# Expert down products ordered chunk by chunk, the further places' products in one run behind, and the end's row loads and register loads reordered

## The chip, the cores and the metric

The kernel runs on one core of a Trainium2 chip, as one program launched once. The metric is the device time in microseconds (us). A core has a matrix engine (PE, with a queue of its own for loading weights, PEld), a vector engine (DVE), a scalar engine (ACT), a general engine (POOL) and a queue that issues transfers (SP); each takes its instructions in its own program order and waits for the others by semaphores. Transfers between the chip's memory (HBM) and the core's buffers run on 16 DMA engines.

## What is computed

One layer on 2048 tokens of 1024 features: two linear-attention mixers, an output projection, and a mixture of experts, with a last normalization. The change touches the experts and the end.

```python
def hier_moe(h, ...):              # h: tokens x 1024, normalized
    # each token goes to its 2 best of the 8 experts in its best of 4 groups
    ...
    def expert_block(args):
        xb, e = args
        return (jax.nn.silu(xb @ w_gate[e]) * (xb @ w_up[e])) @ w_down[e]
    ...
    out = jax.ops.segment_sum(ys * row_w[:, None], row_tok, num_segments=n_tok)

x = x + hier_moe(rmsnorm(x, ln2_w), ...)
return rmsnorm(x, ln_f_w)
```

There are 32 experts. `w_gate` and `w_up` are 1024 x 512 each, `w_down` is 512 x 1024, all in 32-bit floats.

## The kernel before

The stages ahead of the experts (mixers, output projection, routing) end at about 1780 us and are the same in both kernels. They leave the normalized tokens in HBM as two 16-bit halves (`sH`), the residual rows (`sX2`), and for each expert a list of its tokens.

**Precision.** Each 32-bit factor is held as a high and a low 16-bit half, and a product is three matmuls: high x high, high x low, low x high.

**Weights.** `weights_of` (L1292 to L1306) brings an expert's weights in six pieces of 1 MB: gate 0 and 1, up 0 and 1, down 0 and 1. A piece is loaded by SP into one of four buffers `wr` (L1299) and split in two steps: ACT writes the high half into `whl` (L120), DVE the low half (L121), which needs ACT's. The `whl` pieces go round fourteen buffers of 8 KB per partition, six in one pool and eight in another. While PE works on one expert, ACT and DVE split the next one's pieces.

**Places.** An expert has 160 places: 128 in a tile `xg` and 32 further ones in `xg2`, where a token's row lies as four quarters on four partitions. Both are gathered by POOL (L1376, L1380). A token beyond 160 would go to a loop behind the experts (`overflow()` prepares it at expert 3; in this data the loop's body is not run).

**One expert** (`expert`, L1383 to L1449):

- tr: PE transposes the tokens (L1393, and L1401 for `xg2`); ACT copies the high halves into `hTm`, DVE the low ones (L1395, L1402).
- gu: for each of four chunks m of 128 hidden features, 48 matmuls (24 gate, 24 up; L1413) add into one of two buffers `gu`. ACT takes the silu (L1417), DVE multiplies by up (sgm, L1418), ACT writes the high half `ah` (L1419), DVE the low half `al` (L1420).
- dn: for the 128 places, two halves n of 512 output columns, 12 matmuls each (L1429): three products of four chunks. ACT empties n = 0 (L1432), DVE n = 1 (yt, L1434), and POOL scatters `yt` to `sYb` (L1365).
- dr: for the 32 further places, 48 matmuls (L1443), each with 32 columns of weights and 256 moving columns; four of them, for the four quarters of the output, lie side by side in the array. ACT empties them into `yr` (L1447), POOL scatters them.

**What sets the order.** The loop (L1482 to L1493) calls `expert(e)` as a generator and pulls pieces of `weights_of(e + 1)` between its steps. A scheduler then orders the instructions of each engine by a timeline model of its own, among all that depend on nothing unfinished. `tc.issue_after(i)` tells it to place what follows behind instruction i on the engine's queue. So dn and dr of one expert are mixed with tr and gu of the next.

**The end.** When all experts are placed, the weights' buffers are freed, and eight tiles `xr` of the residual (1 MB each, two tiles of 128 tokens) and the last norm's weights `lfb` are loaded into their place (L1501 to L1504). Then each engine loads the overflow loop's count into a register (`values_load`, L1511) and comes to the loop's branch (L1512), at which the engines and the transfers are waited for. Behind it `summed` and `finish` read both expert results of each token (`yf`, L1530, 16 loads of 1 MB), add them to `xr` on DVE (L1532, L1533), normalize (L1535, L1540) and write the result.

Of the kernel before, what the change touches and what calls it, by code (L numbers as in the profile page):

```python
# [9 lines left out]
F32 = mybir.dt.float32  # L10
# [3 lines left out]
AF = mybir.ActivationFunctionType  # L14
# [6 lines left out]
D = 1024  # L21
NT = T // 128
# [22 lines left out]
def tile_kernel(ctx, tc, I, out, dbg=None, stop=99):  # L45
    nc = tc.nc
    V, S, G, P = nc.vector, nc.scalar, nc.gpsimd, nc.tensor
# [19 lines left out]
    sX2 = dram.tile([NT, 128, D], F32, name="sX2")  # L67
# [175 lines left out]
    with pool("p0", 2) as p0:  # L243
# [13 lines left out]
        for t in range(NT):  # L257
# [24 lines left out]
            if t == TV:  # L282

                rows = p0.tile([NV, 128], F32, name="vrows", bufs=1)
                for nme, n in VECS:
                    o = VOFF[nme]
                    a = I[nme]
# [516 lines left out]
    f, b = slice(0, 64), slice(64, 128)  # L804
# [487 lines left out]
    def weights_of(e, res, dyn=False):  # L1292


        for i, (nme, kt) in enumerate((("moe_w_gate", 4), ("moe_w_up", 4), ("moe_w_down", 2))):
            src = I[nme][0, e] if not dyn else I[nme][0, bass.ds(e, 1)].rearrange("o k f -> (o k) f")
            for c in range(2):
                wr = mp["wq"].tile([128, 2048], F32, name="wr")
                nc.sync.dma_start(wr.rearrange("p (k f) -> p k f", k=kt),  # L1299
                                  src[c * kt * 128:(c + 1) * kt * 128, :].rearrange("(k p) f -> p k f" if i == 2 else "(p k) f -> p k f", p=128))  # L1300
                whl = mp["wsp"][next(wpl) % len(mp["wsp"])].tile([128, 2, 2048], F16, name="whl")
                wh, wl = whl[:, 0], whl[:, 1]
                for q in range(2):
                    o = slice(1024 * q, 1024 * q + 1024)
                    split(wh[:, o], wl[:, o], wr[:, o])
                    yield  # L1306
                res.append(tuple(z.rearrange("p (k f) -> p k f", k=kt) for z in (wh, wl)))

    wts = []
# [32 lines left out]
    if True:  # L1342
# [5 lines left out]
        def tokens(dst, src):  # L1348
            V.tensor_scalar(dst, src, T - 1, None, op0=ALU.bitwise_and)
# [12 lines left out]
        ysc = []  # L1362

        def scatter(dst, ix, src, bound):
            ins = G.indirect_dma_start(out=dst, out_offset=bass.IndirectOffsetOnAxis(ap=ix, axis=0), in_=src, in_offset=None,  # L1365
                                       bounds_check=bound, oob_is_err=False)
            for o in ysc:
                tc.declare_no_dep(ins.ins, o.ins, reason="rows of different places")
            ysc.append(ins)

        last = {}
# [11 lines left out]
        def expert(wts, xs, sc, sc2=None):  # L1383

            xg, x2 = xs
            nt = 128 if x2 is None else 160
            hT = mw.tile([128, 2, 8, 160], F16, name="hTm")
            for a in range(2):
                for kq in range(2):
                    pt = ms.tile([128, 4, 128], F16, name="tr")  # L1390
                    for k in range(4):
                        c = a * D + kq * 512
                        P.transpose(pt[:, k, :], xg[:, c + k:c + 512:4], idh)  # L1393
                    o = hT[:, a, kq * 4:kq * 4 + 4, 0:128]
                    ins = S.activation(o, pt, AF.Copy) if a == 0 else V.tensor_copy(o, pt)  # L1395
                last["AV"[a]] = ins.ins
                if a == 0 and x2 is not None:

                    pt = ms.tile([128, 4, 128], F16, name="tr")
                    for j in range(4):  # L1400
                        P.transpose(pt[:, j, :], x2[:, j::4], idh)  # L1401
                    last["A"] = S.activation(hT.rearrange("p a (g j) t -> p (a g) j t", j=4)[:, :, :, 128:160],  # L1402
                                             pt.rearrange("p j (q r) -> p q j r", r=32), AF.Copy).ins
                yield
            ah = mw.tile([128, 4, 160], F16, name="ah")
            al = mw.tile([128, 4, 160], F16, name="al")
            for m in range(4):
                pg = ms.tile([128, 2, 160], F32, name="gu")
                for i in range(2):
                    j = 0  # L1410
                    for a, hf in ((0, 0), (0, 1), (1, 0)):
                        for k in range(8):
                            P.matmul(pg[:, i, 0:nt], wts[2 * i + k // 4][a][:, k % 4, m * 128:(m + 1) * 128], hT[:, hf, k, 0:nt],  # L1413
                                     start=(j == 0), stop=(j == 23))
                            j += 1
                sg = mw.tile([128, 160], F32, name="sgm")
                S.activation(sg[:, 0:nt], pg[:, 0, 0:nt], AF.Silu, scale=IS2)  # L1417
                V.scalar_tensor_tensor(sg[:, 0:nt], pg[:, 1, 0:nt], IS2 * ASC, sg[:, 0:nt], op0=ALU.mult, op1=ALU.mult)  # L1418
                last["A"] = S.activation(ah[:, m, 0:nt], sg[:, 0:nt], AF.Copy).ins  # L1419
                last["V"] = V.tensor_tensor(al[:, m, 0:nt], sg[:, 0:nt], ah[:, m, 0:nt], op=ALU.subtract).ins  # L1420
                yield
            ym = cq.tile([128, 2, NP, 128], F32, name="yt").rearrange("p d q t -> p (d q t)")
            dn = 1.0 / (ASC * SW)
            for n in range(2):
                pd = ms.tile([128, 512], F32, name="dn")
                j = 0
                for a, b in ((ah, 0), (al, 0), (ah, 1)):
                    for m in range(4):
                        P.matmul(pd, a[:, m, 0:128], wts[4 + m // 2][b][:, m % 2, n * 512:(n + 1) * 512], start=(j == 0), stop=(j == 11))  # L1429
                        j += 1  # L1430
                if n == 0:
                    last["A"] = S.activation(ym[:, 0:512], pd, AF.Copy, scale=dn).ins  # L1432
                else:
                    last["V"] = V.tensor_scalar(ym[:, 512:1024], pd, dn, None, op0=ALU.mult).ins  # L1434
                yield
            scatter(sYb[:, :], sc, ym, 2 * T - 1)
            if x2 is not None:
                pd = ms.tile([128, 256], F32, name="dr", bufs=1)
                j = 0
                for a, b in ((ah, 0), (al, 0), (ah, 1)):  # L1440
                    for m in range(4):
                        for n in range(4):
                            P.matmul(pd[32 * n:32 * n + 32, :], a[:, m, 128:160], wts[4 + m // 2][b][:, m % 2, n * 256:(n + 1) * 256],  # L1443
                                     start=(j == 0), stop=(j == 11), skip_group_check=True)
                        j += 1
                yr = mw.tile([128, 256], F32, name="yr")
                S.activation(yr, pd, AF.Copy, scale=dn)  # L1447
                scatter(sY4, sc2, yr, 8 * T - 1)
            yield  # L1449

# [31 lines left out]
        for e in range(32):  # L1482
# [9 lines left out]
            wts = nxt  # L1492
# [3 lines left out]
        p6.close()  # L1496

        fx = p5.enter_context(pool("fx"))
        xr = []
        lfb = fx.tile([128, D], F32, name="lfb")  # L1500
        nc.sync.dma_start(lfb, bcast(I["ln_f_w"], D))  # L1501
        for t in range(0, NT, 2):
            xr.append(fx.tile([128, 2, D], F32, name=f"xr{t}"))
            load = nc.sync.dma_start(xr[-1], sX2[t:t + 2].rearrange("t p d -> p t d"))  # L1504


        with ExitStack() as p7:
            mp["wq"] = p7.enter_context(pool("wqo", 2))
            mp["wsp"] = [p7.enter_context(pool("wspo", 6))]
            with tc.issue_after(load.ins):  # L1510
                nbr = nc.values_load(ovl[0:1, 2, 0:1], min_val=0, max_val=63)  # L1511
            with tc.For_i(0, nbr, 1) as iv:  # L1512
                er = nc.values_load(ovl[0:1, 0, bass.ds(iv, 1)], min_val=0, max_val=31)
                br = nc.values_load(ovl[0:1, 1, bass.ds(iv, 1)], min_val=0, max_val=NSLOT - 128)
                ido = mw.tile([128, 1], I32, name="ido")
                nc.sync.dma_start(ido, sT[bass.ds(br, 128), bass.ds(er, 1)])
                tko = mw.tile([128, 1], I32, name="tko")
                tokens(tko, ido)
                wts = []
                for _ in weights_of(er, wts, True):  # L1520
                    pass
                for _ in expert(wts, gather(tko), ido):
                    pass
# [57 lines left out]
```

## Time and profile before

| | |
|---|---|
| runs | 2589.75, 2592.13, 2596.44 us; median 2592.13 |
| the profiled execution | 2596.26 us, of which the trace spans 2594.5 |
| instructions | 57329 |
| mean granted TensorE clock | 0.913 |
| from HBM / to HBM | 420.94 MB / 168.66 MB |
| expert loop, from its first gate product to the last dr | 1782.97 to 2503.80 us |
| end, from there to the last instruction | 2503.80 to 2594.5 us |
| chain that ended last, largest parts | PE gu 12%, PE dn 4%, ACT whl 3%, DVE whl 3%, PE dr 1% |

A row of a timeline has the start in us, the duration, the engine (SPq is SP's issuing), the line, the operation, output<-input, the shape, and how many instructions the row holds; in brackets stands how long the engine was idle before it, and who ended that. Matmuls are pipelined and their ends are modelled, so the time of a matmul is best read from one start to the next.

### The profile page before, as it was taken

How to read it: one execution, taken by the hardware profiler on the slowest of the kernel's cores; microseconds unless marked ns; L12 is line 12 of the kernel's file. 1: busy time of each engine (PE TensorE's matmuls, PEld its weight loads, DVE VectorE, ACT ScalarE, POOL GpSimd, SP SyncE). 2: the span in 40 equal slices, each digit the busy share in tenths (PEclk: the TensorE clock that was granted, in tenths of full speed). 3: DMA queues.
4: the chain of work that ended last, by engine and by line, in shares of the span. 5: the costliest groups of instructions: out<-in, count | busy, mean ns of one | idle time of the engine just before them, and what ended most of it. 6: DMA issues, size and time to landing. Idle time of an engine off the chain costs nothing. (4 is left out here: it accounts for less than half of the span.)

```text
span 2594.5 us, 57329 instructions
## 1 busy us (share of the span) xinstructions
PE 2199.5 (85%) x22841; PEld 1454.6 (56%) x22841; DVE 1822.1 (70%) x3386; ACT 1307.7 (50%) x2290; POOL 585.8 (23%) x736
## 2 busy tenths in 40 slices
PE   6998887777788989889787998996989999999950
PEld 4444444444444454456675555455877887877740
DVE  7547789777977435645866576684877877777749
ACT  6656464455542144312344434443766777777733
POOL 2323323233311011211101232233222222222110
PEclk8999898889889989989788999997999999999985
DMA  5446676576676749699988685363889999999978
GB/s 179 122 122 178 163 182 172 141 182 166 173 182 166 169 110 225 175 229 248 283 240 242 197 252 156 118 260 122 320 305 326 345 340 343 342 345 348 337 274 341
DMA packets 475455, 591.49 MB, mean 228 GB/s; under 512 B 172177, under 2 KB 363940, under 8 KB 458800
## 3 DMA queue, kind: packets, MB, share of 16 engines
q1 hardware_dynamic: 402656, 444.05, 56.0%
q10 hardware_dynamic: 58768, 105.90, 13.9%
q0 software_dynamic: 13760, 37.83, 3.8%
q8 instruction: 182, 2.98, 0.5%
q14 instruction: 89, 0.73, 0.1%
HBM read 420.94 MB, written 168.66 MB: 227 GB/s over the span
## 5 line engine op out<-in xcount | busy, mean ns | idle before, releaser
L121 DVE SCALAR_TENSOR_TENSOR whl<-wr,whl 128x1024 f16<-128x1024 f32 x384 | 454.3, 1226 | 56.5 <-ACT whl L120 55.1
L1413 PE MATMUL gu<-hTm,whl 128*128 128x160 f16 x6144 | 456.9, 234 | 14.5 <-DVE sgm L1418 11.1
L1413 PEld LDWEIGHTS <-whl 128*128 128x128 f16 x6144 | 431.8, 99 | 28.9 <-issue 21.1
L120 ACT ACTIVATE whl<-wr 128x1024 f16<-128x1024 f32 x384 | 380.6, 1043 | 15.1 <-DMA wr<-in_moe_w_gate_dram 6.8
L145 PEld LDWEIGHTS <-wsh 128*128 128x128 f16 x1472 | 147.7, 102 | 205.9 <-issue 60.7
L145 PE MATMUL ip<-xh,wsh 128*128 128x512 f16 x736 | 198.2, 407 | 22.6 <-ACT ch L176 8.9
L145 PE MATMUL ip<-xh,wsl 128*128 128x512 f16 x736 | 188.7, 391 | 0.0
L145 PE MATMUL ip<-xl,wsh 128*128 128x512 f16 x736 | 185.9, 390 | 0.0
L732 POOL TENSOR_TENSOR uv<-uv,fd 64x512 f32<-64x512 f32 x62 | 70.9, 1143 | 407.3 <-DVE uv L755 258.0
L1429 PE MATMUL dn<-whl,ah 128*128 128x512 f16 x512 | 142.3, 379 | 0.0
L361 PE MATMUL gr<-O 64*128 64x128 f32 x1024 | 88.4, 310 | 53.4 <-DVE O L343 47.4
L145 PEld LDWEIGHTS <-wsl 128*128 128x128 f16 x736 | 72.2, 100 | 86.6 <-issue 10.5
L405 DVE TENSOR_TENSOR tb<-wb,qb 128x31 f32<-128x31 f32 (+15 forms) x248 | 97.0, 391 | 33.0 <-DMA wb<-sW 28.1
L361 PEld LDWEIGHTS gr<-O 64*128 64x128 f32 x1024 | 72.3, 207 | 84.3 <-DVE O L343 59.7
L406 DVE TENSOR_TENSOR qb<-qb,tb 128x31 f32<-128x31 f32 (+15 forms) x248 | 99.9, 403 | 5.4 <-DVE tb L405 0.2
L1419 ACT ACTIVATE ah<-sgm 128x160 f16<-128x160 f32 x128 | 42.6, 333 | 118.1 <-DVE sgm L1418 117.5
L1380 POOL DMA_INDIRECT xg<-sH,tkq x32 | 42.2, 1319 | 249.3 <-PE tr L1401 188.6
L1365 POOL DMA_INDIRECT sYb<-yt,ids x32 | 41.8, 1306 | 237.2 <-ACT whl L120 223.0
L363 DVE TENSOR_TENSOR gt<-gr,mG 128x512 f32<-128x512 f32 x128 | 83.5, 681 | 16.3 <-PE gr L361 14.1
L376 POOL TENSOR_TENSOR bks<-O,fdec 128x512 f32<-128x512 f32 x64 | 77.3, 1207 | 38.8 <-DVE O L343 31.4
L1232 PEld LDWEIGHTS <-mh 128*128 128x128 f16 x512 | 49.8, 101 | 62.7 <-issue 6.8
L332 ACT ACTIVATE EP<-L 128x256 f32<-128x256 f32 x64 | 26.6, 416 | 105.3 <-DVE L L326 105.1
(392 smaller groups left out, 4558.5 us busy)
## 6 DMA issues: line engine op xcount, KB each, us to landing
wr<-in_moe_w_gate_dram SPq DMA_DIRECT2D x64, 1024.0 KB
wr<-in_moe_w_up_dram SPq DMA_DIRECT2D x64, 1024.0 KB
wr<-in_moe_w_down_dram SPq DMA_DIRECT2D x64, 1024.0 KB
sG<-gt SPq DMA_DIRECT2D x64, 512.0 KB
sAR<-O SPq DMA_DIRECT2D x128, 128.0 KB
sBT<-bt SPq DMA_DIRECT2D x64, 256.0 KB
yf<-sYb SPq DMA_DIRECT2D x16, 1024.0 KB
wr<-in_w_in_dram SPq DMA_DIRECT2D x62, 256.0 KB
```

The lines of the kernel that those rows point to most:

```text
L120: S.activation(wh, src, AF.Copy, scale=SW)
L121: V.scalar_tensor_tensor(wl, src, SW, wh, op0=ALU.mult, op1=ALU.subtract)
L145: P.matmul(ps, w[:, k, :], xx[:, k, o], start=(i + k == 0), stop=(i == 2 and k == 7))
L361: P.matmul(pgs[hh][:, c, :], O[rr, c, 0:2, :], O[rr, c, 2:4, :], start=True, stop=True)
L363: V.tensor_tensor(gt[:, :, hh, :], pgs[hh], mG[d][:, None, :].to_broadcast([128, 4, 128]), op=ALU.mult)
L376: G.tensor_tensor(bks, O[:, :, 0:2, :].rearrange("p c a t -> p c (a t)"), fdec[:, d, pi, f0:f0 + 4].unsqueeze(2).to_broadcast([128, 4, 128 ...
L405: V.tensor_tensor(t_, wb[:, ra, u:u + 1].to_broadcast([128, m, n]), qb[:, u:u + 1, ca].to_broadcast([128, m, n]), op=ALU.mult)
L406: V.tensor_tensor(qb[:, ra, ca], qb[:, ra, ca], t_, op=ALU.add)
L732: G.tensor_tensor(cur["uv"][d][BR[d]], uv[d][BR[d]], fd[BR[d], :, fcol(d, s)].unsqueeze(2).to_broadcast([64, 8, 64]), op=ALU.mult)
L1232: P.matmul(ps, a[:, k, :], w[:, k, n * 512:(n + 1) * 512], start=(i + j == 0), stop=(i == 2 and j == 7))
L1413: P.matmul(pg[:, i, 0:nt], wts[2 * i + k // 4][a][:, k % 4, m * 128:(m + 1) * 128], hT[:, hf, k, 0:nt], start=(j == 0), stop=(j == 23))
L1429: P.matmul(pd, a[:, m, 0:128], wts[4 + m // 2][b][:, m % 2, n * 512:(n + 1) * 512], start=(j == 0), stop=(j == 11))
```

## The change

Four things are changed, all shown in the diff below.

1. dn: in each half n, the loop over the four chunks is now outside and that over the three products inside, with low x high last. The chunk-0 products of a half can so be done as soon as chunk 0 is there, its low half included.
2. dr: the same order, and all 48 stand behind the expert's last dn (`issue_after(dl)`).
3. The end's loads: `xr` of tiles 8 to 15 first, then 0 to 7, then `lfb`. All eight `xr` tiles are allocated ahead of `lfb`, so that `lfb` no longer lies before them.
4. `values_load` ahead of the overflow loop now stands behind the last scatter on POOL and behind the last emptying of dr on ACT, as well as behind the last load on SP.

```diff
@@ -1424,9 +1424,9 @@
             for n in range(2):
                 pd = ms.tile([128, 512], F32, name="dn")
                 j = 0
-                for a, b in ((ah, 0), (al, 0), (ah, 1)):
-                    for m in range(4):
-                        P.matmul(pd, a[:, m, 0:128], wts[4 + m // 2][b][:, m % 2, n * 512:(n + 1) * 512], start=(j == 0), stop=(j == 11))
+                for m in range(4):
+                    for a, b in ((ah, 0), (ah, 1), (al, 0)):
+                        dl = P.matmul(pd, a[:, m, 0:128], wts[4 + m // 2][b][:, m % 2, n * 512:(n + 1) * 512], start=(j == 0), stop=(j == 11)).ins
                         j += 1
                 if n == 0:
                     last["A"] = S.activation(ym[:, 0:512], pd, AF.Copy, scale=dn).ins
@@ -1437,14 +1437,15 @@
             if x2 is not None:
                 pd = ms.tile([128, 256], F32, name="dr", bufs=1)
                 j = 0
-                for a, b in ((ah, 0), (al, 0), (ah, 1)):
+                with tc.issue_after(dl):
                     for m in range(4):
-                        for n in range(4):
-                            P.matmul(pd[32 * n:32 * n + 32, :], a[:, m, 128:160], wts[4 + m // 2][b][:, m % 2, n * 256:(n + 1) * 256],
-                                     start=(j == 0), stop=(j == 11), skip_group_check=True)
-                        j += 1
+                        for a, b in ((ah, 0), (ah, 1), (al, 0)):
+                            for n in range(4):
+                                P.matmul(pd[32 * n:32 * n + 32, :], a[:, m, 128:160], wts[4 + m // 2][b][:, m % 2, n * 256:(n + 1) * 256],
+                                         start=(j == 0), stop=(j == 11), skip_group_check=True)
+                            j += 1
                 yr = mw.tile([128, 256], F32, name="yr")
-                S.activation(yr, pd, AF.Copy, scale=dn)
+                last["R"] = S.activation(yr, pd, AF.Copy, scale=dn).ins
                 scatter(sY4, sc2, yr, 8 * T - 1)
             yield
 
@@ -1496,18 +1497,18 @@
         p6.close()
 
         fx = p5.enter_context(pool("fx"))
-        xr = []
+        xr = [fx.tile([128, 2, D], F32, name=f"xr{t}") for t in range(0, NT, 2)]
         lfb = fx.tile([128, D], F32, name="lfb")
+
+        for t in (8, 10, 12, 14, 0, 2, 4, 6):
+            load = nc.sync.dma_start(xr[t // 2], sX2[t:t + 2].rearrange("t p d -> p t d"))
         nc.sync.dma_start(lfb, bcast(I["ln_f_w"], D))
-        for t in range(0, NT, 2):
-            xr.append(fx.tile([128, 2, D], F32, name=f"xr{t}"))
-            load = nc.sync.dma_start(xr[-1], sX2[t:t + 2].rearrange("t p d -> p t d"))
 
 
         with ExitStack() as p7:
             mp["wq"] = p7.enter_context(pool("wqo", 2))
             mp["wsp"] = [p7.enter_context(pool("wspo", 6))]
-            with tc.issue_after(load.ins):
-            with tc.issue_after(load.ins):
+            with tc.issue_after(load.ins), tc.issue_after(ysc[-1].ins), tc.issue_after(last["R"]):
                 nbr = nc.values_load(ovl[0:1, 2, 0:1], min_val=0, max_val=63)
```

The scheduler orders the engines anew from the first expert on. In a late expert before the change, PE runs gu of chunks 2 and 3, 4 dn, 8 dr, 5 tr, 3 gu of the next expert, 2 dn, 4 dr, 27 gu, 7 tr, 14 gu, 18 dn, 36 dr, 18 gu, 34 gu, 8 tr. Of the change it runs, from expert 12 on: gu of chunks 0 and 1 in turns (12, 12, then 36, 36), gu of chunk 2, 6 dn, 4 tr, gu of chunk 3, 12 dn, 8 tr, 6 dn, 48 dr, 4 tr; no gu of the next expert stands ahead of dr. (Experts 4 to 10 still have some.) The last expert runs its four chunks, then 24 dn and 48 dr.

PE before, at the first place in an expert where dr begins, and at the next: a line of rows that only repeat is left out as "...". `whl` are weights, `ah` and `al` the halves of the hidden values, `xg` the next expert's tokens.

```order
L1413 MATMUL gu<-hTm,whl 128x160
L1429 LDWEIGHTS ah
L1429 MATMUL dn<-whl,ah 128x512
...
L1443 LDWEIGHTS ah
L1443 MATMUL dr<-whl,ah 32x256
...
L1393 LDWEIGHTS xg
L1393 MATMUL tr<-idh,xg 128x128
...
L1413 LDWEIGHTS whl
L1413 MATMUL gu<-hTm,whl 128x160
```

PE in the change, from the last gu of an expert to the first of the next:

```order
L1413 MATMUL gu<-hTm,whl 128x160
L1429 LDWEIGHTS ah
L1429 MATMUL dn<-whl,ah 128x512
...
L1429 LDWEIGHTS al
L1429 MATMUL dn<-whl,al 128x512
...
L1444 LDWEIGHTS ah
L1444 MATMUL dr<-whl,ah 32x256
...
L1393 LDWEIGHTS xg
L1393 MATMUL tr<-idh,xg 128x128
...
L1413 LDWEIGHTS whl
```

What moved: the short pieces of dr between gu and tr are gone, dn of the low halves comes early with its chunk, and dr follows dn once.

DVE before, from sgm of chunk 3 of a late expert to al of chunk 0 of the next (L1418 sgm, L1420 al, L121 a split of weights, L1434 yt, L1395 the copy into `hTm`):

```order
L1418 SCALAR_TENSOR_TENSOR sgm<-gu,sgm 128x160
L1420 TENSOR_TENSOR al<-sgm,ah 128x160
L121 SCALAR_TENSOR_TENSOR whl<-wr,whl 128x1024 x2
L1434 TENSOR_SCALAR yt<-dn 128x512
L121 SCALAR_TENSOR_TENSOR whl<-wr,whl 128x1024 x4
L1418 SCALAR_TENSOR_TENSOR sgm<-gu,sgm 128x160
L1395 COPY hTm<-tr 128x4x128
L1418 SCALAR_TENSOR_TENSOR sgm<-gu,sgm 128x160
L1395 COPY hTm<-tr 128x4x128
L1420 TENSOR_TENSOR al<-sgm,ah 128x160
```

DVE in the change, the same stretch:

```order
L1418 SCALAR_TENSOR_TENSOR sgm<-gu,sgm 128x160
L1420 TENSOR_TENSOR al<-sgm,ah 128x160
L1395 COPY hTm<-tr 128x4x128
L121 SCALAR_TENSOR_TENSOR whl<-wr,whl 128x1024
L1434 TENSOR_SCALAR yt<-dn 128x512
L121 SCALAR_TENSOR_TENSOR whl<-wr,whl 128x1024
L1395 COPY hTm<-tr 128x4x128
L121 SCALAR_TENSOR_TENSOR whl<-wr,whl 128x1024 x4
L1418 SCALAR_TENSOR_TENSOR sgm<-gu,sgm 128x160
L1420 TENSOR_TENSOR al<-sgm,ah 128x160
```

What moved: both copies into `hTm` went from between the sgm of chunks 0 and 1 to behind al of chunk 3, one split went from ahead of yt to behind it, and each chunk's sgm and al now stand together with two splits behind them.

SP before, at the end, with what each load waits for (PE, DVE and Pool are those engines' counts, DMAHW are earlier loads on the same channel; the number in a name tells tiles apart):

```order
L1501 DMA lfb_30423<-in_ln_f_w_dram 128x1024 [waits DMAHW1_49,DVE_49]
L1504 DMA xr0_30425<-sX2_78 128x2x1024 [waits DMAHW0_49]
L1504 DMA xr2_30427<-sX2_78 128x2x1024 [waits DMAHW7_49]
L1504 DMA xr4_30429<-sX2_78 128x2x1024 [waits DMAHW6_49]
L1504 DMA xr6_30431<-sX2_78 128x2x1024 [waits PE_49]
L1504 DMA xr8_30433<-sX2_78 128x2x1024 [waits PE_49]
L1504 DMA xr10_30435<-sX2_78 128x2x1024 [waits Pool_49]
L1504 DMA xr12_30437<-sX2_78 128x2x1024
L1504 DMA xr14_30439<-sX2_78 128x2x1024 [waits DMAHW2_49]
L1511 TENSOR_LOAD ovl_9480 [waits DVE_49]
```

SP in the change:

```order
L1504 DMA xr8_30427<-sX2_78 128x2x1024 [waits PE_49]
L1504 DMA xr10_30428<-sX2_78 128x2x1024 [waits PE_49]
L1504 DMA xr12_30429<-sX2_78 128x2x1024 [waits Pool_49]
L1504 DMA xr14_30430<-sX2_78 128x2x1024
L1504 DMA xr0_30423<-sX2_78 128x2x1024 [waits DMAHW6_49,DMAHW1_49,DVE_49]
L1504 DMA xr2_30424<-sX2_78 128x2x1024 [waits DMAHW7_49,DMAHW0_49]
L1504 DMA xr4_30425<-sX2_78 128x2x1024
L1504 DMA xr6_30426<-sX2_78 128x2x1024
L1505 DMA lfb_30431<-in_ln_f_w_dram 128x1024 [waits DMAHW2_49]
L1512 TENSOR_LOAD ovl_9480 [waits DVE_49]
```

What moved: the wait for DVE (the last split, which frees the last `wr` buffer) went from the head of the queue to the fifth place, and two waits for PE to the head. Each `xr` tile now lies exactly over one buffer of the weights: xr0 to xr6 over `wr`, xr8 over up 1 of the expert before the last, xr10 over gate 1 of the last expert, xr12 over its gate 0, xr14 over a down piece of the one before. xr8's wait is for the last gu of the expert before the last, xr10's for the last matmul that reads gate 1 of the last expert, the 24th of chunk 3. On ACT, the last emptying of dr now stands ahead of the loop's branch, on POOL the last scatter ahead of the register load; before, both stood behind the branch.

## The prediction

> **What bounds the kernel now.** I read the page's totals first, then the windows of 22 us, since the kernel has stages and the change touches only the last two: the expert loop (about 1783 to 2504 us) and the end (to 2594.5).
>
> ```profile
> PE 2199.5 (85%) x22841; PEld 1454.6 (56%) x22841; DVE 1822.1 (70%) x3386; ACT 1307.7 (50%) x2290; POOL 585.8 (23%) x736
> 1870.00:1892.00 22.00, 17.32 (x221) 13.28 (x219) 21.92 (x22) 12.11 (x20) 7.53 (x4) 0.94 0.69 244
> 2244.00:2266.00 22.00, 21.69 (x292) 17.65 (x284) 17.36 (x24) 15.87 (x26) 4.75 (x4) 1.00 0.92 342
> ```
>
> A window's row gives busy PE, PEld, DVE, ACT, POOL, then the granted clock, the DMA share and GB/s. In the late loop PE is busy 21.69 of 22 us at full clock, DVE 17.36, and DMA 0.92 x 22 = 20.2 us. PE bounds, but not by much. Early in the loop (1870) it does not: DVE is full there with the work of `overflow()`.
>
> The chain that ended last, cut at the same place of each expert, gives the period.
>
> ```profile
> 1782.97 5.73 PE gu L1413 x52
> 1981.64 4.26 PE gu L1413 x60
> 2112.06 4.05 PE gu L1413 x57
> 2138.47 6.80 PE gu L1413 x96
> 2468.97 6.80 PE gu L1413 x96
> ```
>
> Experts 0 to 7 take (1981.64 - 1782.97) / 8 = 24.8 us each: fill, `overflow()` and DMA waits. Experts 8 to 13 take (2112.06 - 1981.64) / 6 = 21.74. From the third chunk of expert 15 to that of expert 30, (2468.97 - 2138.47) / 15 = 22.03. I call 8 to 13 the middle (six experts) and 14 to 30 the late part (seventeen).
>
> **The change on PE.** One late expert's end in PE's timeline:
>
> ```profile
> 2255.27 1.03 PE L1429 MATMUL dn<-whl,ah 128*128 128x512 f16 x4
> 2256.23 0.40 PE L1443 MATMUL dr<-whl,ah 128*32 128x256 f16 x8
> 2256.56 0.47 PE L1393 MATMUL tr<-idh,xg 128*128 128x128 f16 x5
> ...
> 2257.60 0.29 PE L1443 MATMUL dr<-whl,ah 128*32 128x256 f16 x4
> 2257.83 2.04 PE L1413 MATMUL gu<-hTm,whl 128*128 128x160 f16 x27
> ...
> 2262.57 1.03 PE L1429 MATMUL dn<-whl,ah 128*128 128x512 f16 x4
> 2263.44 0.81 PE L1429 MATMUL dn<-whl,al 128*128 128x512 f16 x3
> ...
> 2265.04 0.29 PE L1443 MATMUL dr<-whl,ah 128*32 128x256 f16 x4
> 2265.16 0.61 PE L1443 MATMUL dr<-whl,al 128*32 128x256 f16 x16
> 2265.60 0.61 PE L1443 MATMUL dr<-whl,ah 128*32 128x256 f16 x16
> 2266.14 3.77 PE L1413 MATMUL gu<-hTm,whl 128*128 128x160 f16 x52
> 2269.75 0.61 PE L1393 MATMUL tr<-idh,xg 128*128 128x128 f16 x8
> 2270.67 1.54 PE L1413 MATMUL gu<-hTm,whl 128*128 128x160 f16 x20 [0.31 <-DVE sgm L1418]
> ```
>
> Ends are modelled, so I go from start to start. Four dn take 0.87 (2262.57 to 2263.44), 0.217 each, but 0.96 where dr follows (2255.27 to 2256.23): entering a piece of dr costs 0.09. Sixteen dr inside a piece take 0.44 (2265.16 to 2265.60), 0.0275 each; the pieces of 8, 4 and 36 take 0.33, 0.23 and 1.10, together 1.66. With three entries that is 1.93 us. In one run: the 36 take 1.10, twelve more 0.33, one entry 0.09, so 1.52. **Saved: 0.41 us an expert.** Matmul counts are the same. Which weight half goes first inside a sum changes no count either; I take it at nothing, since each matmul already has a weight load of its own that hides under it.
>
> Secondly, eight tr from 2269.75 should end after 8 x 0.056 = 0.45 (the 0.61 is seven steps and one 0.22), yet gu goes on only 0.92 later: PE loses 0.48, waiting for DVE's read of chunk 0's sums (the gu tile has two buffers, and chunk 2 wants the first). In the change chunk 0 is done 36 gu, 36 x 0.0694 = 2.5 us (0.0694 = (2269.75 - 2266.14) / 52), ahead of chunk 2, so this wait should go: 0.48, in the late experts alone. PE by itself would then need 22.03 - 0.41 - 0.48 = 21.14 us.
>
> **What is late next.** Splits of weights and the three small steps of a chunk stand in one queue on DVE, and each split there waits for ACT's half. That makes a ring, chunk to chunk, with no PE in it. Its steps in DVE's timeline, and ACT's two rows that matter:
>
> ```profile
> 2248.49 0.42 DVE L1395 COPY hTm<-tr 128x512 f16<-128x512 f16 x1
> 2254.72 0.32 DVE L1418 SCALAR_TENSOR_TENSOR sgm<-gu,sgm 128x160 f32<-128x160 f32 x1
> 2256.38 1.22 DVE L121 SCALAR_TENSOR_TENSOR whl<-wr,whl 128x1024 f16<-128x1024 f32 x1 [0.62 <-ACT whl L120]
> 2257.78 1.23 DVE L121 SCALAR_TENSOR_TENSOR whl<-wr,whl 128x1024 f16<-128x1024 f32 x1 [0.18 <-ACT whl L120]
> 2258.93 0.32 DVE L1418 SCALAR_TENSOR_TENSOR sgm<-gu,sgm 128x160 f32<-128x160 f32 x1
> 2260.59 2.36 DVE L121 SCALAR_TENSOR_TENSOR whl<-wr,whl 128x1024 f16<-128x1024 f32 x2 [0.62 <-ACT whl L120]
> 2265.15 0.69 DVE L1434 TENSOR_SCALAR yt<-dn 128x512 f32<-128x512 f32 x1 [2.19 <-PE dn L1429]
> 2265.76 4.62 DVE L121 SCALAR_TENSOR_TENSOR whl<-wr,whl 128x1024 f16<-128x1024 f32 x4
> 2270.30 0.32 DVE L1418 SCALAR_TENSOR_TENSOR sgm<-gu,sgm 128x160 f32<-128x160 f32 x1
> ...
> 2256.69 1.06 ACT L120 ACTIVATE whl<-wr 128x1024 f16<-128x1024 f32 x1 [0.34 <-DMA wr<-in_moe_w_up_dram]
> 2259.28 0.34 ACT L1419 ACTIVATE ah<-sgm 128x160 f16<-128x160 f32 x1 [0.85 <-DVE sgm L1418]
> ```
>
> From one sgm to the next is 2258.93 - 2254.72 = 4.21, of which 0.26 is the split at 2257.78 that started late (1.14 after the one at 2256.38 would be 2257.52) because ACT waited for a piece of weights; 3.95 without it. By DVE's new order (the section on the change): three such steps, 11.85; then sgm of chunk 3 to its split 1.66 (2258.93 to 2260.59), split 1.14, yt 0.61 (2265.15 to 2265.76), split 1.14, hTm 0.42, four splits 4.54 (2265.76 to 2270.30). The other hTm falls into the 0.62 that DVE waits for ACT, if its tr is done. Together **21.36, about 21.3** (the last hTm overlaps its neighbour a little). Before, this ring had 2.19 us of air where yt waits for PE's dn; in the change dn ends earlier against DVE's queue and the air is gone. So PE's 21.14 and the ring's 21.3 are nearly equal. The slower one sets the period; I take 21.3. Bounds: 21.14, if the steps overlap more, and 21.6, if each expert has one late piece of weights as at 2256.69 (0.3). DMA needs 20.2 of the 21.3, and its pieces are asked for more evenly than now (no 2.19 pause), so I lean to the ring without that wait.
>
> **The end.**
>
> ```profile
> 2490.00 9.26 SPq L1504 DMA_DIRECT2D xr<-sX  x8
> 2495.04 0.36 SPq L1504 DMA_DIRECT2D xr<-sX  x1
> 2476.00:2488.00 12.00, 12.00 (x147) 8.25 (x146) 7.89 (x10) 7.76 (x12) 1.07 (x1) 1.00 0.26 104
> 2494.00:2514.00 20.00, 9.81 (x111) 5.70 (x108) 1.77 (x5) 1.57 (x4) 0.97 (x1) 0.83 1.02 410
> 2503.10 0.70 PE L1443 MATMUL dr<-whl,ah 128*32 128x256 f16 x16
> 2517.24 0.38 ACT L1447 ACTIVATE yr<-dr 128x256 f32<-128x256 f32 x1 [14.86 <-DMA xr<-sX]
> 2520.15 40.59 SPq L1530 DMA_DIRECT2D yf<-sYb  x16
> ```
>
> PE ends at 2503.80. Then ACT stands at the loop's branch, until the row loads have landed, with the last yr and its scatter behind it; yf starts at 2520.15, 16.35 after PE. The change takes yr and scatter ahead of the branch: the 2.91 us from 2517.24 to 2520.15 go. But DMA is idle meanwhile (share 0.26 in 2476 to 2488), and the new order of loads hardly uses that. xr8 goes first and can start in the hole; the other seven and lfb stand in SP's queue behind xr10, which waits for PE. xr10 lies over the last expert's second gate piece, which chunk 3 reads last. The single issue at 2495.04 above is the old xr8, which lay half over the same piece and waited for the same product, 8.8 before PE's end. In the new order 24 gu, 24 dn and dr follow that product: 1.67 + 5.2 + 1.52 = 8.4 us. Price of the loads: before, 8.9 MB (eight loads and lfb) from 2490.00 to the release at 2517.24 took 27.2; 8.9 MB at 410 GB/s is 21.7, the other 5.5 are start, scatters and loop entry. Now 7.86 MB: 19.2 + 5.5 = 24.7 after xr10's issue, PE's end + 16.3. **End: nothing** (16.3 for 16.35); bounds -1 and +2 us, from how soon the transfers get to full rate.
>
> **The sum.** Middle: 6 x (21.74 - 21.3) = 2.6. Late: 17 x (22.03 - 21.3) = 12.4. At the edges: before, 54 gu of the last expert stand ahead of the dr of the one before it, now none: 54 x 0.0694 = 3.7 come behind; at expert 8 it is 36 against 24, 0.8 back; and the last expert saves its 0.4: together -2.5. Experts 0 to 7 wait for other things than PE: of at most 8 x 0.41 = 3.3 I take 1, with bounds -5 (their order is new too, and four of them lose over 2 us each against the middle now) and +3.3. 2.6 + 12.4 - 2.5 + 1 + 0 = **13.5 us**. The profiled execution took 2596.26 us (span 2594.5), so it would become 2582.8; the runs' median is 2592.13, 4.1 below that execution, so I forecast **2579 us**.
>
> **Rivals.**
> 1. *Ring or weights a little slower.* One late piece per expert as at 2256.69: 23 x 0.3 = 7 us of the gain go, about 2586. For it: the share of 0.92 rises to 20.2 / 21.3 = 0.95. Against: the requests come evenly.
> 2. *Slower: PE stalls at chunk 3's down products.* Now up to 44 gu and the tr stand between chunk 3's last gu and its dn. In the change twelve dn (2.6) and eight tr (0.45) do, 3.05 us. In the rows above chunk 3's gu end at 2255.27, and its ah ends at 2259.62, 4.35 later. If it stays so late, PE stalls 1.3 each time, the period is 22.4, and 23 x 1.1 = 25 us turn the forecast into 2604. It decides from a stall of 0.9 (22.03 - 21.14). Against: ah comes so late because chunk 3's silu and sgm stand behind two splits in a ring with slack; a ring of 21.3 cannot lag further than its own 0.16 beyond PE each time.
> The Trainium skill, "TensorE: Matmul & The Clock Gate", section "Step-by-step: what each phase is for", says that only weight loads are pulled ahead and matmuls stay in program order. By that rule, nothing behind a waiting dn can slip past it, and this rival's stall would be paid in full; the trace agrees at 2270.67, where gu waits and no later matmul starts.
> 3. *The end does gain.* If xr10 did not wait for PE, four loads (4.2 MB, 10 us) would fill the hole; yf would start some 9 us earlier: 2570. For it: the idle DMA. Against: the PE wait that stands at xr10, with six loads and lfb behind it.
>
> **How the numbers follow.** Forecast (gain 8 to 18) 0.60; rival 1 (0 to 8) 0.22; rival 3, or a period of 21.14, (18 to 25) 0.09; rival 2 0.09. A measurement here tells 0.3% from no change, 7.8 us, so the line is at 2584.4: faster 0.69, within 0.23 (rival 1 and a mild rival 2), slower 0.08. Range 2568 to 2590: it takes in both bounds of the period and the end, and leaves out rival 2 and the worst of the early experts.
>
> **What would show it.** Right: periods of 21.2 to 21.4 from expert 8 on, one piece of 48 dr at 1.5, no wait of gu for sgm, small waits of dn (about 0.2) for ah or al, DVE without the 2.19 before yt; yf 16 to 17 us after PE's end. Wrong: late periods over 21.6, ACT rows waiting for DMA in each expert, dn waiting over 0.5, or experts 4 to 10 as slow as 24 us.

## The result and the profile after

The change takes 2575.22 us (median of 13 runs), the kernel before 2595.59 us in the same job (13 runs): ratio 0.9925, 95% interval 0.9912 to 0.9938, some 20 us less. The forecast was 2579.0 us against a median of 2592.13, 13 us less. Run again later on another occasion, the change gave 0.9935 (0.9911 to 0.9960).

The profiled execution spans 2567.8 us, 26.7 less than that of before. Eleven of these are not the change's: the first gu of the loop starts at 1771.95 us instead of 1782.77 (the 1782.97 in the sections ahead is a row of the chain, which begins 0.2 later), and nothing ahead of it was changed; in other executions it came between 1764.7 and 1788.4. From that gu to PE's end, which is the end of its last row, it is 15.4 us less (705.6 for 721.0), and behind PE's end 0.4 (90.3 for 90.7).

The page of the change, engines and the chain that ended last, and below it the chain of before:

```profile
PE 2182.8 (85%) x22841; PEld 1461.7 (57%) x22841; DVE 1825.0 (71%) x3386; ACT 1308.3 (51%) x2290; POOL 580.0 (23%) x736
...
DVE 13%; PE 8%; ACT 6%; DMA 4%; issue 3%; SPq 0%; POOL 0%; DVEq 0%; ACTq 0%
```
```profile
PE 20%; DVE 8%; ACT 4%; DMA 3%; issue 2%; POOL 0%; SPq 0%; POOLq 0%; ACTq 0%; another core or an unknown queue 0%; DVEq 0%
```

Before, PE led the chain with 20% of the span, and DVE and ACT had 12%; now these two have 19% and PE 8%.

The period of an expert is read best from yt, once an expert on DVE. The summary of that line (count, duration in ns, first and last start) for experts 7 to 30, first of before, then of the change:

```profile
L1434 DVE TENSOR_SCALAR yt<-dn x24: 691/692/693, 1980.6 to 2485.5; 128x512 f32<-128x512 f32 x24
```
```profile
L1434 DVE TENSOR_SCALAR yt<-dn x24: 683/684/689, 1964.4 to 2456.3; 128x512 f32<-128x512 f32 x24
```

504.9 / 23 = 21.95 us before, 491.9 / 23 = 21.39 after (the four periods from expert 7 to 11 are faster, 20.8; those from 12 on take 21.51). One late expert of the change in DVE's timeline, from the sgm of chunk 2 to the next sgm of chunk 2, and below the same place in every third expert:

```profile
2362.60 0.32 DVE L1418 SCALAR_TENSOR_TENSOR sgm<-gu,sgm 128x160 f32<-128x160 f32 x1
2363.32 0.33 DVE L1420 TENSOR_TENSOR al<-sgm,ah 128x160 f16<-128x160 f32 x1 [0.40 <-ACT ah L1419]
2364.27 2.36 DVE L121 SCALAR_TENSOR_TENSOR whl<-wr,whl 128x1024 f16<-128x1024 f32 x2 [0.62 <-ACT whl L120]
2366.55 0.32 DVE L1418 SCALAR_TENSOR_TENSOR sgm<-gu,sgm 128x160 f32<-128x160 f32 x1
...
2367.51 0.42 DVE L1395 COPY hTm<-tr 128x512 f16<-128x512 f16 x1
2368.21 1.23 DVE L121 SCALAR_TENSOR_TENSOR whl<-wr,whl 128x1024 f16<-128x1024 f32 x1 [0.28 <-ACT whl L120]
2369.36 0.68 DVE L1434 TENSOR_SCALAR yt<-dn 128x512 f32<-128x512 f32 x1
2369.96 1.22 DVE L121 SCALAR_TENSOR_TENSOR whl<-wr,whl 128x1024 f16<-128x1024 f32 x1
2371.09 0.42 DVE L1395 COPY hTm<-tr 128x512 f16<-128x512 f16 x1
2371.42 4.62 DVE L121 SCALAR_TENSOR_TENSOR whl<-wr,whl 128x1024 f16<-128x1024 f32 x4
2375.96 0.32 DVE L1418 SCALAR_TENSOR_TENSOR sgm<-gu,sgm 128x160 f32<-128x160 f32 x1
...
2383.85 0.32 DVE L1418 SCALAR_TENSOR_TENSOR sgm<-gu,sgm 128x160 f32<-128x160 f32 x1
```
```profile
2323.71 0.32 DVE L1418 SCALAR_TENSOR_TENSOR sgm<-gu,sgm 128x160 f32<-128x160 f32 x1
...
2328.25 0.75 DVE L1395 COPY hTm<-tr 128x512 f16<-128x512 f16 x2
2328.91 4.62 DVE L121 SCALAR_TENSOR_TENSOR whl<-wr,whl 128x1024 f16<-128x1024 f32 x4
2333.45 0.32 DVE L1418 SCALAR_TENSOR_TENSOR sgm<-gu,sgm 128x160 f32<-128x160 f32 x1
```

This is the forecast ring, without a gap that belongs to PE. From sgm to sgm 3.95, three times, and from chunk 3 to the next chunk 0 it is 2375.96 - 2366.55 = 9.41 (forecast 9.51): 2383.85 - 2362.60 = 21.25. The 2.19 us ahead of yt are gone. Where both hTm come behind yt (every third expert), none of them falls into DVE's wait for ACT, and the last leg is 2333.45 - 2323.71 = 9.74, 0.33 more. The floor is thus (2 x 21.25 + 21.58) / 3 = 21.36 us.

PE at the same expert's end, the 48 dr from their first row to the tr behind them, and PE's groups from 2069 to 2457 us (busy, mean ns of one, idle before it and who ended it):

```profile
2368.69 0.40 PE L1444 MATMUL dr<-whl,ah 128*32 128x256 f16 x8
...
2370.11 0.41 PE L1393 MATMUL tr<-idh,xg 128*128 128x128 f16 x4
```
```profile
L1413 PE MATMUL gu<-hTm,whl 128*128 128x160 f16 x3456 | 248.2, 233 | 0.0
L1429 PE MATMUL dn<-whl,ah 128*128 128x512 f16 x288 | 81.9, 380 | 3.9 <-ACT ah L1419 3.5
```

The 48 dr take 1.42 us in one piece (forecast 1.5). gu waits for sgm no more; dn waits for ah, 3.9 / 18 = 0.22 us an expert, about what was forecast. Most of this falls in experts whose weights come late: in the others it is 0.00, 0.18 and 0.07 in turns.

The end of the change: SP's issues, ACT's last product, and windows (busy PE, PEld, DVE, ACT, POOL, then clock, DMA share, GB/s):

```profile
2450.91 22.95 SPq L1504 DMA_DIRECT2D xr<-sX  x8
...
2493.59 3.73 SPq L1531 DMA_DIRECT2D yf<-sYb  x6
```
```profile
2477.60 0.38 ACT L1448 ACTIVATE yr<-dr 128x256 f32<-128x256 f32 x1 [1.06 <-PE dr L1444]
```
```profile
2460.00:2468.00 8.00, 8.00 (x119) 8.00 (x117) 3.46 (x6) 2.16 (x7) 1.00 (x1) 1.00 0.12 47
```

yr no longer waits for the loads, but yf starts 16.0 us behind PE's end (2477.55), nearly as before (16.35), and DMA lies idle at a share of 0.12 ahead of it.

### The profile page after: what moved, and what is told of

It reads as the page before. It is cut to its first block, busy times and chain, and to the rows that moved or that the text cites. A ratio compares the mean times of both kernels' runs of the same rounds, so it can differ in the third digit from the quotient of the medians.

```text
span 2567.8 us, 57328 instructions
## 1 busy us (share of the span) xinstructions
PE 2182.8 (85%) x22841; PEld 1461.7 (57%) x22841; DVE 1825.0 (71%) x3386; ACT 1308.3 (51%) x2290; POOL 580.0 (23%) x736
## 5 line engine op out<-in xcount | busy, mean ns | idle before, releaser
L121 DVE SCALAR_TENSOR_TENSOR whl<-wr,whl 128x1024 f16<-128x1024 f32 x384 | 453.8, 1220 | 75.5 <-ACT whl L120 74.9
L361 PE MATMUL gr<-O 64*128 64x128 f32 x1024 | 88.3, 309 | 53.5 <-DVE O L343 47.9
L1380 POOL DMA_INDIRECT xg<-sH,tkq x32 | 36.6, 1143 | 296.1 <-PE tr L1393 178.3
L1429 PE MATMUL dn<-whl,al 128*128 128x512 f16 x256 | 90.0, 379 | 1.0 <-DVE al L1420 1.0
```

The source lines that it names most:

```text
L121: V.scalar_tensor_tensor(wl, src, SW, wh, op0=ALU.mult, op1=ALU.subtract)
L361: P.matmul(pgs[hh][:, c, :], O[rr, c, 0:2, :], O[rr, c, 2:4, :], start=True, stop=True)
L1429: dl = P.matmul(pd, a[:, m, 0:128], wts[4 + m // 2][b][:, m % 2, n * 512:(n + 1) * 512], start=(j == 0), stop=(j == 11)).ins
```

## The experiments

### Which part brings it

Four kernels on one chip: dn's order alone in the kernel before (`for m ... for a, b` instead of `for a, b ... for m`); dr alone, in one run behind dn, with the order of the sums as before; both; and the end alone.

```diff
# dr alone
-                        P.matmul(pd, a[:, m, 0:128], ...)
+                        dl = P.matmul(pd, a[:, m, 0:128], ...).ins
...
+                with tc.issue_after(dl):
                     for a, b in ((ah, 0), (al, 0), (ah, 1)):
```

> Only the down products' new order (chunk by chunk) in the kernel before; the further places' products stay as they were and stand now in four pieces an expert instead of three; the end is that of before. Theory A (PE's price list of the prediction): the 0.48 us for which gu waits for sgm goes in the late experts, one piece more costs 0.2; 17 x 0.28 = 5 us less, ratio 0.998; late period 21.75, no gu wait on sgm. Rival B (the gain comes from the new order of DVE and ACT, and the pieces of dr cost next to nothing because something else bounds): the period falls to 21.3 here already, ratio 0.993 to 0.994.

> Only the further places' products in one run behind the down products, with the order of both sums as before (first all products of ah with the high half of the weights, then al, then the low half); the end is that of before. Theory A: 0.41 us an expert from fewer pieces, the 0.48 us of gu waiting for sgm stay; (17 + 6) x 0.41 = 9 us less, ratio 0.9965; late period 21.6. Rival B: DVE and ACT keep their old order, so nothing is gained, ratio 0.999 to 1.001, and PE waits elsewhere for what it saves.

> Both changes of the expert loop, the end of before (old order of the row loads, register loads ahead of the last scatter). Theory A (the end brings nothing): 15 to 20 us less than before, ratio 0.9925 to 0.994, the same as the whole change. Rival C (the end does bring some of it): the ratio stays 2 us or more short of the whole change's, above 0.9935, and first yf comes over 18 us behind PE's end.

> Only the end of the change (register loads behind the last scatter, row loads from 8 on first), with the expert loop of before. Theory A: within 2 us of before, ratio 0.999 to 1.001, since the loads behind xr10 still start with PE's end; first yf 16 to 17 us behind PE's end. Rival C: 3 to 9 us less, ratio 0.9965 to 0.999, first yf 13 us or less behind PE's end.

Measured: dn alone 1.0015 (0.9998 to 1.0031), dr alone 1.0011 (0.9998 to 1.0025), both 0.9935 (0.9917 to 0.9954), the end alone 1.0008 (0.9993 to 1.0022). The end brings nothing that these runs can tell (yf 15.45 us behind PE's end with it alone, 15.75 in the kernel with both halves of the loop and the old end). The two halves of the loop bring nothing singly and 17 us together. So the gain is not the sum of what the halves bring alone.

The late stretch of both singles: dn alone, a window of 100 us (PE, PEld, DVE, ACT, POOL) and yt's line over experts 12 to 30; then dr alone, PE's rows at the place where gu waits; then gu's group of before over fifteen experts, with its wait.

```profile
2245.00:2345.00 100.00, 100.00 (x1319) 80.30 (x1318) 80.36 (x106) 74.76 (x117) 22.34 (x20) 1.00 0.94 344
```
```profile
L1434 DVE TENSOR_SCALAR yt<-dn x19: 680/682/692, 2071.5 to 2467.9; 128x512 f32<-128x512 f32 x19
```
```profile
2157.08 0.61 PE L1393 MATMUL tr<-idh,xg 128*128 128x128 f16 x8
2158.29 3.89 PE L1413 MATMUL gu<-hTm,whl 128*128 128x160 f16 x54 [0.60 <-DVE sgm L1418]
```
```profile
L1413 PE MATMUL gu<-hTm,whl 128*128 128x160 f16 x2878 | 211.6, 233 | 4.8 <-DVE sgm L1418 4.8
```

With dn alone, gu's wait is gone and PE is full, with dr in four pieces; the late periods lie between 21.2 and 23.3, and their mean is 396.4 / 18 = 22.02, that of before, where 21.75 was expected. With dr alone, a late expert that nothing disturbs takes 21.87 instead of the expected 21.6: by the rows, gu's wait for sgm grew from 4.8 / 15 = 0.32 to 0.60 us. (A wait in a row counts from a modelled end. From start to start, gu follows the eight tr after 1.21 us here and after 0.92 in the prediction's rows; without the 0.45 that the tr themselves take, PE loses 0.76 here, and 0.48 there.) PE's own time thus did shrink as priced, to 21.87 - 0.76 = 21.11, near the prediction's 21.14, but most of the saving became a wait. Besides, every seventh expert took 24.1 to 24.3 us, with ACT waiting 3.2 to 3.5 us for a piece of weights, so that the mean of experts 12 to 30 is 21.98 against 22.01 before.

### What held the kernel before

The new theory: the late period of before is that of a loop through PE *and* DVE: last dn, yt, four splits, sgm of chunk 0, gu of chunk 2 (which needs the buffer that sgm reads), and on through PE to the next last dn. One DVE operation more behind yt tells it from a bound on PE:

```diff
                     last["V"] = V.tensor_scalar(ym[:, 512:1024], pd, dn, None, op0=ALU.mult).ins
+                    last["V"] = V.tensor_scalar(ym[:, 1024 - 128:1024], pd[:, 512 - 128:512], dn, None, op0=ALU.mult).ins
```

> The kernel before with the same DVE operation more per expert as was added to the change (yt's last 128 columns of the second half written twice; it took 0.19 us of the period there). DVE's queue is otherwise the same from expert 10 on, the operation stands one split behind yt. Theory F (the period of before, 22.03, is that of a loop: PE's last dn, yt, the four splits behind it, sgm of the first chunk, gu of the third chunk, and round through PE): all of it shows, late period 22.2 to 22.25, gu's wait for sgm 0.48 + 0.19, 4 us in all. Theory A as the prediction had it (PE alone sets 22.03, and DVE has 2.19 us of air before yt): late period 22.03.

> The same operation more in the kernel with only dr in one run. Theory F (the same loop holds it at 21.87, which is why it gained next to nothing from 0.41 us less of PE): late period 22.0 to 22.1. Rival H (PE or something else holds it at 21.87): 21.85 to 21.9.

The summaries of yt's line: before, and of the added operation's in the kernel before with it, with gu's group there below; then yt with dr alone, and with dr alone and the operation (five experts, 14 to 18).

```profile
L1434 DVE TENSOR_SCALAR yt<-dn x15: 691/692/693, 2133.0 to 2441.4; 128x512 f32<-128x512 f32 x15
```
```profile
L1435 DVE TENSOR_SCALAR yt<-dn x16: 283/284/286, 2118.0 to 2451.4; 128x128 f32<-128x128 f32 x16
```
```profile
L1413 PE MATMUL gu<-hTm,whl 128*128 128x160 f16 x3138 | 230.6, 233 | 8.1 <-DVE sgm L1418 8.1
```
```profile
L1434 DVE TENSOR_SCALAR yt<-dn x5: 690/691/692, 2109.0 to 2196.6; 128x512 f32<-128x512 f32 x5
```
```profile
L1434 DVE TENSOR_SCALAR yt<-dn x5: 691/692/692, 2120.6 to 2208.9; 128x512 f32<-128x512 f32 x5
```

308.4 / 14 = 22.03 becomes 333.4 / 15 = 22.23, and 87.6 / 4 = 21.90 becomes 88.3 / 4 = 22.08. All of the added 0.2 shows in both, and gu's wait in the first grew by the same, from 0.32 to 8.1 / 16 = 0.51. The ratios, both to the kernel before, are 1.0027 (1.0010 to 1.0043) and 1.0025 (1.0007 to 1.0043); dr alone had 1.0011, and a difference as small as that between the last two is not told apart by the runs, only by the periods. The loop is shown for the late experts: the 5.5 us of DVE between yt and gu (2265.15 to 2270.67 in the prediction's rows) were on the path, and a yt that waits 2.19 us had no air behind it.

It does not hold everywhere. From expert 7 to 13 of before (1980.6 to 2111 us), the periods are 21.65 to 21.80, and none of PE's groups there has a wait, gu included; by these rows PE itself is the bound:

```profile
L1413 PE MATMUL gu<-hTm,whl 128*128 128x160 f16 x1155 | 84.9, 233 | 0.0
```

This also accounts for the singles. dr alone shortens PE's own time, but the loop holds the period at 21.87. dn alone opens the loop, but with four pieces of dr PE's own time holds the period at 22.02 (0.27 more than was priced, which stays open). Only both together get past the two bounds.

### A third buffer for gu

If the buffer is what closes the loop, one more should open it without the new order of dn: `name="gu", bufs=3`, with dr alone.

> The kernel before with dr in one run behind dn (the sums' order as before), and a third buffer for gu's sums, so that the third chunk's gu need not wait until the first chunk's sums are read; its PE and DVE orders differ from both kernels (chunk 0 to 2 in one run of gu). With two buffers this kernel had periods of 21.87, and gu waited 0.74 us an expert for sgm, more than the 0.3 before. Theory F (what held that kernel was a loop through PE's last dn, yt, the splits behind it, sgm and the gu that waits for its buffer; the order chunk by chunk matters because it opens this loop): periods of 21.1 to 21.5, ratio 0.993 to 0.996. Rival G (the order of DVE's queue itself is what counts, with a sgm evenly after each pair of splits): periods stay at 21.8 or above, ratio 0.998 to 1.002, with PE waiting for hTm or sgm elsewhere.

yt's line over experts 8 to 28, and the group of dn in the same stretch:

```profile
L1434 DVE TENSOR_SCALAR yt<-dn x21: 690/691/692, 2001.6 to 2455.5; 128x512 f32<-128x512 f32 x21
```
```profile
L1429 PE MATMUL dn<-whl,ah 128*128 128x512 f16 x320 | 88.9, 380 | 21.8 <-ACT ah L1419 21.8
```

Slower: 1.0037 (1.0020 to 1.0053), the period 453.9 / 20 = 22.70. The expectation of theory F fell: gu of three chunks ran ahead in one piece, and dn stood 21.8 / 20 = 1.1 us an expert waiting for ah. That is rival 2 of the prediction, in another kernel. The third buffer did not replace the order that spreads the chunks; whether it would help under another order of PE isn't shown. The rule that the prediction took from the Trainium skill, "TensorE: Matmul & The Clock Gate", section "Step-by-step: what each phase is for" (matmuls stay in program order), agrees with this trace too: PE starts no later matmul during the 1.1 us.

### What holds the change

The same DVE operation more in the change, and, in another kernel, eight dr more for PE:

```diff
# x_dr3
-                            for n in range(4):
+                            for n in range(4 * (3 if j == 0 else 1)):
+                                n = n % 4
```

> The whole change with one DVE operation more per expert: yt's last 128 columns of the second half are written twice. From expert 11 on the order on PE, ACT and DVE is that of the change's commonest expert, with this one operation behind yt. Theory A (the ring of DVE and ACT sets the period, 21.25): the period grows by all that the operation takes on DVE, 0.15 to 0.25 us, to 21.4 to 21.5, and PE's waits at dn for ah grow by as much. Rival E (PE sets the period): period 21.25 as before, DVE's idle time takes it up.

> The whole change with eight dr products more per expert: the first group of four is computed three times, 8 x 0.0275 = 0.22 us of PE. From expert 11 on the order is nearly that of the change. Theory A (ring of DVE and ACT): the period stays 21.25, and PE's wait at dn for ah, 0.2 to 0.4 us an expert in the change, shrinks by 0.22. Rival E (PE sets the period): 21.47, 5 us in all from expert 8 on.

The added operation takes 0.20 from start to start (2173.59 to 2173.79 in one expert). yt's line over experts 11 to 20, first of this kernel, then of the change:

```profile
L1434 DVE TENSOR_SCALAR yt<-dn x10: 682/683/684, 2064.6 to 2257.6; 128x512 f32<-128x512 f32 x10
```
```profile
L1434 DVE TENSOR_SCALAR yt<-dn x10: 683/684/687, 2047.6 to 2240.7; 128x512 f32<-128x512 f32 x10
```

21.44 in each of these experts (one has 21.46), 21.25 + 0.19: the ring of an expert with the same order, to the hundredth. With the added operation one hTm always falls into the wait, so there is no longer an expert of 21.58, and the floor rises by 0.08 only, from 21.36 to 21.44; PE's wait at dn, 0.14 in each, grew by about as little (0.08 in the change's experts without late weights). That the two means are alike (21.44 and 21.46) is chance: three of the change's nine periods have late weights (0.41 to 0.52 us of ACT's wait), none of this kernel's is longer for it. The ratio is 0.9936 (0.9914 to 0.9959), the change's within the noise.

The eight dr more gave a ratio of 0.9984 (0.9970 to 0.9999), a loss of 13 to 15 us against the change's ratios in other jobs (0.9935 and 0.9925), where none was expected. yt's line over experts 20 to 30 and over three late experts without late weights, with PE's gu and dn groups from 2065 to 2455 us, in this kernel, then the same two lines of yt in the change:

```profile
L1434 DVE TENSOR_SCALAR yt<-dn x11: 680/683/685, 2260.8 to 2476.5; 128x512 f32<-128x512 f32 x11
L1434 DVE TENSOR_SCALAR yt<-dn x4: 680/683/684, 2390.2 to 2454.7; 128x512 f32<-128x512 f32 x4
```
```profile
L1413 PE MATMUL gu<-hTm,whl 128*128 128x160 f16 x3456 | 248.0, 233 | 2.0 <-DVE hTm L1395 1.7 <-issue 0.2
L1429 PE MATMUL dn<-whl,ah 128*128 128x512 f16 x288 | 82.8, 379 | 0.1
```
```profile
L1434 DVE TENSOR_SCALAR yt<-dn x11: 683/683/685, 2240.7 to 2456.3; 128x512 f32<-128x512 f32 x11
L1434 DVE TENSOR_SCALAR yt<-dn x4: 683/683/684, 2326.5 to 2390.6; 128x512 f32<-128x512 f32 x4
```

The late sum looks as theory A expected, 215.7 us for 215.6, and PE's wait at dn went from 0.22 to nothing. But the change's stretch holds one expert of 22.82, in which ACT waits 1.65 us for weights, and this kernel's holds none like it. Where no weights are late, three experts take 64.5 us here and 64.1 in the change (64.55 and 64.09 by their rows): 0.15 more each, about two thirds of the 0.22. PE thus has very little to spare in the change, and theory A's "the period stays" held in part only. One place where it shows is gu, which now waits for hTm (1.7 / 18 = 0.09 an expert, nothing in the change). The larger loss lies where the order still differs: 89.0 us for 83.2 in experts 7 to 11 (1976.2 to 2065.2, and 1964.4 to 2047.6). Of the whole loss the trace shows 8.4 from expert 7 to 30; the rest is open, and so is what a PE longer by more than 0.22 would cost.

### The end, in another order

The loads that needn't wait for the last product first: xr10 and xr12 go last.

```diff
-        for t in (8, 10, 12, 14, 0, 2, 4, 6):
+        for t in (8, 14, 0, 2, 4, 6, 10, 12):
```

> The whole change, with the row loads in another order: 8, 14, 0, 2, 4, 6, then 10, 12 and lfb. Theory A (the end gains nothing because xr10, which waits for PE's last chunk, stands ahead of loads whose place comes free earlier): five loads of 1.05 MB go in the hole, only 2.6 MB stay behind xr10, 6.4 us at 410 GB/s; the first yf comes 6 to 9 us behind PE's end instead of 16.1, and the run is 7 to 10 us shorter than the change alone, ratio to before 0.989 to 0.991. Rival D (the loop's entry sets the end, its waits and branches, or the last scatter): yf stays 14 us or more behind PE, the ratio stays at that of the change, 0.9925 to 0.9935.

> The change itself, beside the next kernel on the same chip. All theories: ratio to before 0.991 to 0.994, first yf 16 us behind PE's end.

> The change with the row loads in the order 8, 14, 0, 2, 4, 6, 10, 12, beside the change on the same chip. Theory A: 6 to 9 us less than the change, ratio to before lower by 0.002 to 0.0035, first yf 8 us behind PE's end. Rival D (the gain seen once was a chance of one job): the same ratio as the change within 0.001.

Measured 0.9897 (0.9870 to 0.9924) first, then beside the change on one chip 0.9893 (0.9869 to 0.9917) against 0.9935 (0.9911 to 0.9960). PE's last row, SP's issues, and the window that was idle, in that second run:

```profile
2477.57 0.28 PE L1444 MATMUL dr<-whl,al 128*32 128x256 f16 x4
```
```profile
2451.22 19.28 SPq L1504 DMA_DIRECT2D xr<-sX  x8
...
2486.12 12.51 SPq L1531 DMA_DIRECT2D yf<-sYb  x8
```
```profile
2461.00:2469.00 8.00, 8.00 (x119) 8.00 (x117) 3.09 (x7) 1.86 (x6) 1.00 (x1) 1.00 0.93 320
```

The hole is filled (0.93 for 0.12), and yf starts 8.3 us behind PE's end, where the change beside it has 16.2. This version beats both kernels: the trace shows 7.9 us less behind PE's end (82.5 for 90.4), as expected (6 to 9), and the medians differ by 11 (2553.49 and 2564.82, six runs each). The 3 us between the two are not accounted for.

## Why the prediction was right, and where it wasn't

- **The time.** 13 us less were forecast, the runs give 17 to 20, the trace 15.9 in what the change touches. What lies between 15.9 and 20 isn't settled; executions differ by as much. That the sum came so near is luck in part: experts 8 to 30 brought 2.0 us less than forecast and experts 0 to 7 3.6 more.
- **"PE bounds, but not by much"** is the step that failed, for the late experts. The prediction read 22.03 as PE's own 21.14 plus 0.41 for pieces and 0.48 of waiting, and gave DVE 2.19 us of air. The added operation showed that the air wasn't there: 0.20 more on DVE were 0.20 more of period. A wait of a few tenths on gu was the mark of the whole loop.
- **0.41 and 0.48 as separate savings** failed with it. As sizes both held: dr alone brought PE's own time to 21.11, and 48 dr take 1.42 us in one piece. But neither comes off the period alone, since the other bound then holds it. The forecast went through unhurt because the change does both at once and its period was taken from the ring.
- **The ring of 21.3 as the next bound** held. The floor is 21.25, in every third expert 21.58: the prediction's condition "if its tr is done" was left open there, and is worth 0.33 in a third of the experts. Experts 8 to 30 brought 504.9 - 491.9 = 13.0 us instead of 15.0; of the 2.0, 1.4 is that 21.3 was taken where the sum of the steps, and the floor, are 21.36 (23 x 0.06).
- **Rival 1** (late weights) was there in part. From expert 12 on the mean is 21.51 (2069.1 to 2456.3 in 18 periods), 0.15 above the floor of 21.36. ACT's wait for weights in that stretch, 3.5 / 18 = 0.19 an expert, where that rival had 0.3:

```profile
L120 ACT ACTIVATE whl<-wr 128x1024 f16<-128x1024 f32 x216 | 214.4, 1046 | 3.5 <-DMA wr<-in_moe_w_gate_dram 2.1 <-DMA wr<-in_moe_w_up_dram 1.3
```

- **Experts 0 to 7** were the mis-sized term. From the first gu (1782.77 and 1771.95) to yt of expert 7 it is 197.8 us before and 192.5 after, 5.4 less, where 1 + 0.8 were taken and 3.3 was the bound. PE's waits in that stretch fell by 2.5: 9.1 at gu and 5.3 at tr before, 8.1 and 2.8 after, with 1.0 new at dn. The prediction didn't look at those of tr. The rest, 2.9, is PE's own time, near the 8 x 0.41 that was the bound. PE's groups, before (1782 to 1981) and after (1772 to 1965):

```profile
L1413 PE MATMUL gu<-hTm,whl 128*128 128x160 f16 x1572 | 121.3, 239 | 9.1 <-DVE sgm L1418 5.8 <-issue 3.4
L1393 PE MATMUL tr<-idh,xg 128*128 128x128 f16 x138 | 13.8, 224 | 5.3 <-ACT hTm L1402 4.7 <-ACT hTm L1395 0.5
```
```profile
L1413 PE MATMUL gu<-hTm,whl 128*128 128x160 f16 x1560 | 122.6, 242 | 8.1 <-issue 3.5 <-DVE sgm L1418 2.8 <-DVE hTm L1395 1.8
L1393 PE MATMUL tr<-idh,xg 128*128 128x128 f16 x130 | 11.9, 221 | 2.8 <-DVE hTm L1395 1.7 <-ACT hTm L1395 0.7 <-ACT hTm L1402 0.5
```

  The size itself isn't settled: another execution of the old loop had 190.3 (the end alone), others of the new one 183.2 (both halves) and 185.9 (the change again). One and the same loop thus differs from itself by more than the 5.4.

- **The last expert's edge** came out at 2.9 for 3.3: yt of expert 30 to PE's end is 18.3 us before and 21.2 after.
- **The end** held, by its reason: not the register loads but xr10's place in the queue. Rival 3's condition, met by another order, is worth 8 us, near the 9 that were put on it.
- **Rival 2** did not happen here, and happened in the kernel with the third buffer.

## What to carry to other kernels

An engine that is busy for 21.7 of 22 us isn't yet the bound: a wait of a few tenths on it, for an engine that itself waits for it, can mark a loop, and then the loop's length is what counts. Add a small operation of known length to the engine that seems to have air; if the period grows by all of it, there was none. Read that from single periods with the same order of instructions, since a sum also holds late weights and other orders. Where loads into freed buffers stand in one queue, put those first whose buffers come free first.

## What had not been expected

Two edits that gain nothing singly (1.0015 and 1.0011) gained 0.65% together. And an operation of 0.2 us added in every expert of the change raised the floor by 0.08 only, since it moved a copy into a wait that was there anyway.
